# Order of the short sequence's attention blocks, stepwise block ends, and stores issued by POOL, in a one-layer bidirectional encoder

## The chip, the cores and the metric

The kernel runs on one core of one Trainium2 chip. The metric is the device time of one execution in microseconds (us); the median of several runs is given. The core has five engines that take their own instruction streams: PE (TensorE, matrix products, with its weight loads shown as PEld), DVE (VectorE), ACT (ScalarE), POOL (GpSimd) and SP (SyncE, which here only issues transfers). Transfers (DMA) are issued from the queues of SP, ACT and POOL. Engines wait for each other through semaphores.

## What is computed

One layer of a hybrid encoder over two sequences of 2048 and 256 positions with the same weights, in float32. Eight mLSTM heads (both directions) and eight attention heads (two key/value groups of four query heads) share one input projection:

```python
h = rmsnorm(x, norm1_w)
p = h @ w_in                       # mq, mk, mv, mo, gates, aq, ak, av
m_out = mlstm_mixer(mq, mk, mv, mo, gates, b_gates, mh_norm_w)
a_out = attention_mixer(aq, ak, av, q_norm_w, k_norm_w)
x = x + jnp.concatenate([m_out, a_out], axis=-1) @ w_out
h = rmsnorm(x, norm2_w)
a, g = jnp.split(centred_dwconv(h @ w_up, conv_w, conv_b), 2, axis=-1)
x = x + (jax.nn.silu(g) * a) @ w_down          # then a final rmsnorm
```

Attention is softmax(q k / 8) v without a mask, each sequence by itself. D = 1024, head width 64, feed-forward width 2816.

## The kernel before

Positions are cut into 18 tiles of 128: tiles 0 to 15 are the long sequence, 16 and 17 the short one. Every float32 product is made of two or three faster products of split operands: a "hi" part, and a "lo" part that holds what is left (DVE computes it as the difference).

Four stages follow each other. First comes the norm and the projection of what attention and the gates need (to about 260 us). Then attention and mLSTM run interleaved; when mLSTM is at its end (about 1385 us) the output projection with `w_out` takes its place beside attention (`phase_c`: nine blocks of 256 positions, each 192 matmuls `po`). Last comes the feed-forward part, from about 1870 us. The order of the instructions on each engine is fixed when the program is built: the kernel is written as generators that yield between steps, `run_both` takes steps of attention and of mLSTM by their cost, and a scheduler that comes with the language then places each engine's instructions by its own simulation of time. So an edit in one generator shifts instructions of others.

Attention (L461 to L677) works in 36 blocks, listed in `hbs`: a block is 512 queries (four tiles) of one key/value group. In group 0 a large block is four tiles of one head of the long sequence (16 blocks); in group 1 it is two tiles of two heads (16 blocks). Each group has two short blocks: both tiles of the short sequence for two heads. A large block passes over 16 key tiles in eight steps `kp` of two tiles, a short one over two key tiles in one step. Per block:

- `prep` (L529): loads the rotated queries (`bq`, by SP), turns them on PE (`pq`) and copies them to `qq` and `qm`.
- `maxstep` (L553): one matmul `px` of a query tile with up to 512 keys and its row maximum on DVE (`mx`, L558); 16 of them for a large block, 4 for a short one. `prep2` (L560) then writes the negative maximum into `qm`, through a PE transposition `pr`.
- `scores` (L573): per key tile two matmuls `ps`, two exponentials on ACT (`ph` L584, `ps` L585) and the lo part on DVE (`pl`, L586).
- `values` (L590): six matmuls into `pv`, two steps behind `scores`.
- `fin1` (L601): ACT copies `pv` to `o1` and `rs`. `fin2` (L610), four times: DVE takes the reciprocal of 128 columns of `rs`. `fin3` (L617): POOL multiplies and stores the block to `mix_d` (two stores for two heads, one for one). `fin4`: marks query tiles as done, which `run_both` asks before it hands out a block of the output projection.

While block n runs, block n+1 (`nxt`) is prepared, and block n−1 (`old`) is ended: one `fin2` per step, `fin3` at the sixth step, `fin4` at the last. A short block has one step, in which all four `fin2`, `fin3`, `fin4` of `old` and all of the preparation of the next block stand.

`mlstm` takes its heads in four pairs. `weights` (L692) loads eight tiles of 128×512 for pairs 1 to 3 (`rm`, SP), and ACT (L105) and DVE (L109) split each into hi and lo. Raw tiles come from two pools of two buffers. Its recurrence reads rows that were stored earlier (`dm`, POOL's loads from `nm_d`, with DMB buffers, L821).

`phase_c` (L960 to L1042): `loads` fetches the mixed heads (`cmx`, L988, split by ACT L989 and DVE L990) and x (`cx`, L994) by SP. `mm` makes `po` (L1003). `post` adds x (DVE, L1008), stores x1 (L1009, called `x_d` in the profile), and sums squares (ACT L1011, POOL L1013, `cacc`). `tail` makes the norm (DVE L1020) and stores it (L1022, `n_d`). In `loads`, `post` and `tail` SP issues all transfers, in program order. The last two blocks need the last attention block's output.

The feed-forward part reads `n_d` again (`rn`, `n`, `nt`, L1069 to L1090), loads the up weights (`ru`, L1103, split at L1115 and L1116; POOL's `tw`, L1124 to L1127, combines them), and multiplies on PE (`pa`, `pb`, `pc`, L1119).

Of the kernel before, what the change touches and what calls it, by code (L numbers as in the profile page):

```python
# [17 lines left out]
P = 128  # L18
# [6 lines left out]
HD = 64  # L25
# [30 lines left out]
WB = 8  # L56
RST = 512
QZB = 2
RWM = 4
S1B = 2  # L60
DMB = 6
KWB = 2
CSTEP = 1
LEAD = 1.3
# [47 lines left out]
def load_split(g, hi, lo, src, pool, name, step, col=None, bufs=2):  # L112

    n = src.shape[-1]
    for k in range(0, n, step):
        r = pool.tile([P, step], F32, tag="raw", name=f"{name}_{k}", bufs=bufs)
        split(g, hi[:, k:k + step], lo[:, k:k + step], src[:, k:k + step], r, col)
# [343 lines left out]
def attention(g, tc, s1, s2, pp):  # L461
# [5 lines left out]
    for grp in range(2):  # L467
        h0 = 4 * grp
        small = [(grp, [(h, 16, 18) for h in (hh, hh + 1)], 16, 18) for hh in (h0, h0 + 2)]
        if grp == 0:  # L470
            hbs += small + [(grp, [(h, 4 * b, 4 * b + 4)], 0, 16) for b in range(4) for h in range(h0, h0 + 4)]
        else:

            large = [(grp, [(h, 2 * b, 2 * b + 2) for h in (hh, hh + 1)], 0, 16) for b in range(8)
                     for hh in (h0, h0 + 2)]
            hbs += large[0:8] + small + large[8:]
    kv = {}

    def load_kv(grp, k0, k1, after=None):
# [49 lines left out]
    def prep(n):  # L529

        s = HB()
        grp, s.qs, k0, k1 = hbs[n]
        load_q(n)
        load_q(n + 1)
        load_kv(grp, k0, k1)
        s.kv = kv[(grp, k0)]
        s.nq, s.nk = 4, k1 - k0
        s.N = s.nq * P
        s.nm = "%d_%d" % s.qs[0][0:2]
        qz = qzs.pop(n)  # L540
        pq = pp.tile([P, 512], F32R, tag="sc", name="pq" + s.nm)
        for t in range(s.nq):
            nc.tensor.transpose(pq[:, t * P:(t + 1) * P], qz[:, t, :], g.identr)
        s.qq = sp.tile([P, 512], F32R, tag="qq", name="qq" + s.nm, bufs=2)
        nc.scalar.activation(s.qq[:, 0:s.N], f32(pq[:, 0:s.N]), AF.Copy)
        s.qm = sp.tile([65, 512], F32R, tag="qm", name="qm" + s.nm, bufs=2)
        nc.scalar.activation(s.qm[0:HD, 0:s.N], f32(pq[0:HD, 0:s.N]), AF.Copy)
        s.mx = sp.tile([P, 4, 4], F32, tag="mx", name="mx" + s.nm, bufs=2)
        s.nsp = -(-s.nk * P // 512)
        s.todo = [(t, z) for z in range(s.nsp) for t in range(s.nq)]  # L550
        return s

    def maxstep(s):  # L553
        t, z0 = s.todo.pop(0)
        w = min(512, s.nk * P - z0 * 512)
        ps = pp.tile([P, 512], F32, tag="sc", name=f"px{s.nm}_{t}_{z0}")
        nc.tensor.matmul(ps[:, 0:w], s.qq[:, t * P:(t + 1) * P], s.kv[z0][0][:, 0:w], start=True, stop=True)  # L557
        nc.vector.tensor_reduce(s.mx[:, t, z0:z0 + 1], ps[:, 0:w], AX.X, ALU.max)  # L558

    def prep2(s):  # L560

        nq = s.nq
        s.m4 = sp.tile([P, 4], F32, tag="m4", name="m4" + s.nm, bufs=2)
        nc.vector.tensor_reduce(s.m4[:, 0:nq], s.mx[:, 0:nq, 0:s.nsp], AX.X, ALU.max)
        m4r = sp.tile([P, 4], F32R, tag="m4r", name="m4r" + s.nm, bufs=2)
        nc.vector.tensor_scalar(m4r[:, 0:nq], s.m4[:, 0:nq], -1.0, None, ALU.mult)
        pr = pp.tile([P, 512], F32, tag="sc", name="pr" + s.nm)
        for t in range(nq):
            nc.tensor.matmul(pr[:, t * P:(t + 1) * P], m4r[:, t:t + 1].to_broadcast([P, P]), g.identr, start=True,
                             stop=True)  # L570
        nc.scalar.activation(s.qm[HD:HD + 1, 0:s.N], pr[HD:HD + 1, 0:s.N], AF.Copy)
# [29 lines left out]
    def fin1(s):  # L601

        N = s.N
        s.o1 = sp.tile([HD, 512], F32, tag="o1", name="o1" + s.nm, bufs=2)
        s.rs = sp.tile([HD, 512], F32, tag="rs", name="rs" + s.nm, bufs=1)
        nc.scalar.activation(s.o1[:, 0:N], s.pv[0:HD, 0:N], AF.Copy)
        nc.scalar.activation(s.rs[:, 0:N], s.pv[HD:P, 0:N], AF.Copy)
        s.left = list(range(0, N, P))

    def fin2(s):  # L610

        if s.left:
            r = s.rs[:, s.left[0]:s.left[0] + P]
            s.left.pop(0)
            nc.vector.reciprocal(r, r)

    def fin3(s):  # L617
        N = s.N
        nc.gpsimd.tensor_tensor(s.o1[:, 0:N], s.o1[:, 0:N], s.rs[:, 0:N], ALU.mult)
        for t0, (h, q0, q1) in part(s):  # L620
            r0 = HD * (h % 2)
            nc.gpsimd.dma_start(g.mix_d[q0 // 2:q1 // 2, r0:r0 + HD, 4 + h // 2].rearrange("n p t -> p n t"),
                                s.o1[:, t0 * P:(t0 + q1 - q0) * P].rearrange("p (n t) -> p n t", t=BT))

    def fin4(s):

        for h, q0, q1 in s.qs:
            if h == 7:
                g.mixed.update(range(q0, q1))
# [4 lines left out]
        yield 0.5  # L634
    prep2(cur)
    load_kv(0, 0, NT1, cur.m4)
    old = None
    for n in range(len(hbs)):
        nxt = prep(n + 1) if n + 1 < len(hbs) else None
        nkp = cur.nk // 2  # L640
        todo = []
        for kp in range(nkp):
            todo.append(scores(cur, kp))
            if kp >= PLAG:
                values(cur, *todo.pop(0))
            if nxt is not None and nxt.todo:
                if n == len(hbs) // 2 - 1:

                    k = 2 * (kp - 2) - (nxt.nq * nxt.nsp - len(nxt.todo))
                else:  # L650
                    k = -(-len(nxt.todo) // max(nkp - kp - MXE, 1))
                for _ in range(k):
                    maxstep(nxt)
                if not nxt.todo:
                    prep2(nxt)
            if old is not None:
                for _ in range(1 if kp < nkp - 1 else 4):
                    fin2(old)
                if kp == min(5, nkp - 1):
                    fin3(old)  # L660
                if kp == nkp - 1:
                    fin4(old)
                    old = None
            yield 2.2
        for t in todo:
            values(cur, *t)
        fin1(cur)
        yield 1
        if nxt is not None and nxt.todo:
            while nxt.todo:  # L670
                maxstep(nxt)
            prep2(nxt)
        old, cur = cur, nxt
    for _ in range(4):
        fin2(old)
    fin3(old)
    fin4(old)  # L677


def mlstm(g, tc, s1, sp, sw, sn, pj_, pm):  # L680
# [11 lines left out]
    def weights(p):  # L692
        s = Pair()
        s.p = p
        s.hs = slice(2 * p, 2 * p + 2)
        s.w = [sw.tile([P, 2, 512], F32R, tag="w", name=f"wm{p}_{c}", bufs=WB) for c in range(NCC)] if p else g.wm0
        for c in range(NCC if p else 0):
            load_split(g, s.w[c][:, 0, :], s.w[c][:, 1, :], g.w_m[p, c], g.raw if c % RWM < 2 else sp,
                       f"rm{p}_{c}", RST, g.n1w[:, c:c + 1], bufs=2 if c % RWM < 2 else RWM - 2)
        s.kT, s.qb, s.va, s.C, s.kw = [], [], [], [], {}  # L700
        for i in range(NT):
            s.C.append(sp.tile([P, 2, 65], F32, tag="C", name=f"C{p}_{i}", bufs=NT))
        for b in range(NB):
            s.kT.append(s1.tile([P, BT], F32, tag="kT", name=f"mkT{p}_{b}", bufs=NB))
            s.qb.append(s1.tile([P, 2, 2, P], F32, tag="qb", name=f"qb{p}_{b}", bufs=NB))
            s.va.append(s1.tile([P, 2, 2, 65], F32, tag="va", name=f"va{p}_{b}", bufs=NB))
        return s
# [252 lines left out]
def phase_c(g, sn, sp, pp, wps):  # L960
# [45 lines left out]

    def post(b, z, x, po, acc):
        nc.vector.tensor_tensor(x[z], po, x[z], ALU.add)  # L1008
        g.st.dma_start(g.x1_d[b, :, 2 * z:2 * z + 2], x[z])  # L1009
        q = acc if z == 0 else sp.tile([P, 2, BT], F32, tag="sq", name=f"csq{b}_{z}", bufs=1)  # L1010
        nc.scalar.activation(q, x[z], AF.Square, scale=1.0 / 32.0)  # L1011
        if z:
            nc.gpsimd.tensor_tensor(acc, acc, q, ALU.add)  # L1013

    def tail(b, x, acc):
        nc.gpsimd.tensor_tensor(acc[:, 0], acc[:, 0], acc[:, 1], ALU.add)
        r = rstd_bc(g, sp, pp, [acc[:, 0]], BT, "r", f"c{b}")
        for z in range(4):
            for o in range(2):
                nc.vector.scalar_tensor_tensor(x[z][:, o], x[z][:, o], g.n2w[:, 2 * z + o:2 * z + o + 1],  # L1020
                                               r, ALU.mult, ALU.mult)
            g.st.dma_start(g.n2_d[:, 2 * z:2 * z + 2, b * BT:(b + 1) * BT], x[z])  # L1022
        g.normed.add(b)

    for c in range(NCC):
# [491 lines left out]
```

## Time and profile before

| | us |
|---|---|
| runs, median of 3 (lowest, highest) | 3474.17 (3474.0, 3474.66) |
| the profiled execution: its own time | 3475.05 |
| its span in the profile | 3473.3 |
| PE busy in it | 3346.2 |
| DVE busy | 2670.5 |
| POOL busy | 1103.9 |

The profile is of one execution. Its own time is 1.75 us above its span. Views used below: the page itself; windows (busy time of each engine in a stretch of time, then the number of instructions in brackets); waits (which line of an engine waited for which other engine's line: total us, times, longest); groups (instructions of one line, one operation and one shape, with their number, total and mean in ns); transfers (number, KB, median us from issue to landing); and the timeline. In a name such as `po<-cmx,wo` the output stands left of the arrow.

### The profile page before, as it was taken

How to read it: one execution, taken by the hardware profiler on the slowest of the kernel's cores; microseconds unless marked ns; L12 is line 12 of the kernel's file. 1: busy time of each engine (PE TensorE's matmuls, PEld its weight loads, DVE VectorE, ACT ScalarE, POOL GpSimd, SP SyncE). 2: the span in 40 equal slices, each digit the busy share in tenths (PEclk: the TensorE clock that was granted, in tenths of full speed). 3: DMA queues.
4: the chain of work that ended last, by engine and by line, in shares of the span. 5: the costliest groups of instructions: out<-in, count | busy, mean ns of one | idle time of the engine just before them, and what ended most of it. 6: DMA issues, size and time to landing. Idle time of an engine off the chain costs nothing. (4 is left out here: it accounts for less than half of the span.)

```text
span 3473.3 us, 55765 instructions
## 1 busy us (share of the span) xinstructions
PE 3346.2 (96%) x20058; PEld 3103.0 (89%) x20058; DVE 2670.5 (77%) x4654; ACT 1930.9 (56%) x4329; POOL 1103.9 (32%) x1328
## 2 busy tenths in 40 slices
PE   7989999999999999999988999999999999999998
PEld 6878888888888887987778999999999998999998
DVE  6875687677777789767666888888888878887776
ACT  4536566666666766645554444446544446555555
POOL 6643133222224322211116233225333224322222
PEclk9999999999999999999999999999999999999999
DMA  6765334343355443432218233223333223421221
GB/s 222 238 197 162 117 107 118 104 131 101 105 169 161 131 144 115 145 105 70 68 51 296 73 97 98 74 65 130 127 105 99 67 73 119 145 65 63 73 73 50
DMA packets 258501, 404.29 MB, mean 116 GB/s; under 512 B 33552, under 2 KB 158256, under 8 KB 258224
## 3 DMA queue, kind: packets, MB, share of 16 engines
q1 hardware_dynamic: 230320, 358.24, 32.3%
q0 software_dynamic: 11344, 33.04, 3.5%
q10 hardware_dynamic: 16560, 9.44, 0.9%
q8 instruction: 158, 2.59, 0.3%
q14 instruction: 119, 0.97, 0.1%
HBM read 316.73 MB, written 83.90 MB: 115 GB/s over the span
## 5 line engine op out<-in xcount | busy, mean ns | idle before, releaser
L1257 PE MATMUL pd<-act,wd 128*128 128x384 f32 (+1 forms) x3120 | 593.2, 336 | 25.2 <-DVE acc L1259 14.4
L1257 PEld LDWEIGHTS pd<-act,wd 128*128 128x128 f32 x3120 | 539.5, 189 | 34.0 <-DVE acc L1259 20.0
L586 DVE TENSOR_TENSOR pl<-ps,ph 128x512 fp32r<-128x512 f32 x520 | 354.1, 685 | 235.3 <-ACT ps L585 228.2
L1119 PE MATMUL pa<-nt,wut 128*128 128x386 f32 (+2 forms) x2376 | 454.5, 339 | 2.0 <-DVE nt L1071 2.0
L1119 PEld LDWEIGHTS pa<-nt,wut 128*128 128x128 f32 x2376 | 421.4, 190 | 2.3 <-DVE nt L1071 2.3
L584 ACT ACTIVATE ph<-ps 128x512 fp32r<-128x512 f32 x520 | 309.7, 596 | 177.1 <-PE ps L581 172.3
L558 DVE TENSOR_REDUCE mx<-px 128x1 f32<-128x512 f32 (+1 forms) x528 | 343.8, 671 | 67.4 <-PE px L557 65.4
L1213 DVE SCALAR_TENSOR_TENSOR y<-u,cw,y 128x768 f32<-128x768 f32 (+1 forms) x264 | 314.0, 1190 | 36.3 <-ACT y L1206 29.2
L598 PE MATMUL pv<-ph,v 128*128 128x512 f32 (+1 forms) x1040 | 330.2, 405 | 2.9 <-ACT ph L584 2.4
L1124 POOL TENSOR_TENSOR tw<-ru 128x512 f32<-128x512 f32 x66 | 91.1, 1380 | 744.4 <-DMA ru<-w_up 573.3
L1135 ACT ACTIVATE u<-pa 128x386 f32<-128x386 f32 (+2 forms) x264 | 128.4, 486 | 328.4 <-PE pa L1119 326.9
L585 ACT ACTIVATE ps<-ps 128x512 f32<-128x512 f32 x520 | 310.9, 599 | 0.0
L1259 DVE TENSOR_TENSOR acc<-pd,acc 128x384 f32<-128x384 f32 (+1 forms) x544 | 280.6, 536 | 34.5 <-PE pd L1257 33.5
L1003 PEld LDWEIGHTS po<-cmx,wo 128*128 128x128 f32 x1728 | 233.9, 191 | 32.6 <-ACT cmx L989 16.2
L1003 PE MATMUL po<-cmx,wo 128*128 128x256 f32 x1728 | 242.2, 284 | 14.9 <-ACT cmx L989 14.8
L580 PE MATMUL ps<-qq,kk 128*128 128x512 f32 x520 | 217.0, 421 | 1.8 <-DVE pl L586 1.1
L557 PE MATMUL px<-kk,qq 128*128 128x512 f32 (+1 forms) x528 | 207.7, 411 | 6.6 <-DVE pl L586 3.5
L598 PE MATMUL pv<-pl,v 128*128 128x512 f32 x520 | 206.6, 407 | 6.9 <-DVE pl L586 6.6
L581 PE MATMUL ps<-qm,kl 65*128 65x512 f32 x520 | 209.1, 405 | 0.0
L724 PE MATMUL mj<-mn,wm 128*128 128x256 f32 x1296 | 197.4, 288 | 3.5 <-ACT og L738 2.1
L724 PEld LDWEIGHTS mj<-mn,wm 128*128 128x128 f32 x1296 | 182.1, 192 | 17.6 <-ACT og L738 2.5
L734 PE MATMUL mv<-wm,mn 128*128 128x256 f32 x1296 | 196.2, 288 | 1.1 <-ACT qb L730 0.9
(288 smaller groups left out, 7239.0 us busy)
## 6 DMA issues: line engine op xcount, KB each, us to landing
ru<-w_up SPq DMA_DIRECT2D x132, 512.0 KB, 3.4
mn<-n_d SPq DMA_DIRECT2D x216, 256.0 KB, 3.3
rd<-w_down SPq DMA_DIRECT2D x66, 512.0 KB, 3.6
n_d<-n1T SPq DMA_DIRECT2D x18, 1024.0 KB, 5.6
dm<-nm_d POOLq DMA_DIRECT2D x72, 256.0 KB, 4.0
mjn<-n_d SPq DMA_DIRECT2D x72, 256.0 KB, 3.3
mvn<-n_d SPq DMA_DIRECT2D x72, 256.0 KB, 3.2
q_d<-qz SPq DMA_DIRECT2D x18, 512.0 KB, 3.5
```

The costliest lines, as they stand in the source:

```text
L558: nc.vector.tensor_reduce(s.mx[:, t, z0:z0 + 1], ps[:, 0:w], AX.X, ALU.max)
L580: nc.tensor.matmul(ps, kk[:, kc:kc + P], s.qq[:, 0:N], start=True, stop=False)
L584: nc.scalar.activation(ph, ps, AF.Exp)
L585: nc.scalar.activation(ps, ps, AF.Exp)
L586: nc.vector.tensor_tensor(pl, ps, f32(ph), ALU.subtract)
L598: nc.tensor.matmul(s.pv[0:HD if k in (1, 3) else P, 0:N], v, p, start=(kp == 0 and k == 0), stop=(2 * kp + 2 == s.nk and k == 5))
L724: nc.tensor.matmul(pj[:, o], s.w[c][:, a, o * P:(o + 1) * P], nT[c][:, :, h, :], start=(c + o + k == 0), stop=(c == NCC - 1 and k == 2 and ...
L1003: nc.tensor.matmul(po[:, o], wo[c][z // 2][:, a, n], mx[c][:, h, :], start=(c == 0 and k == 0), stop=(c == NCC - 1 and k == 2))
L1119: nc.tensor.matmul(p, w[:, aa, c, :], ops[k][:, c, bb, 0:n], start=c == 0 and i == 0 and not add, stop=c == NCC // 2 - 1 and i == 2, skip_ ...
L1213: nc.vector.scalar_tensor_tensor(y[:, s:e], u[:, s + k:e + k], cw[:, k, jj:jj + 1], y[:, s:e], ALU.mult, ALU.add)
L1257: nc.tensor.matmul(po, wds[j][c // 4][:, aa, c % 4 * P:(c % 4 + 1) * P], acts[j][:, bb, z0:z1], start=(j == 0 and k == 0), stop=(j == len( ...
L1259: nc.vector.tensor_tensor(accs[c][:, z0:z1], po, accs[c][:, z0:z1], ALU.add)
```

## The change

The list `hbs` now has single short blocks between large ones. In group 0: short, large, short, then the other 15 large. In group 1: six large, short, two large, short, the other eight large. A list `ready` holds the prepared blocks; when the next block is short and the current one large, the block after the next is prepared too, both within the current block's steps. The block ends become a list `ends` of six steps per block (four `fin2`, `fin3`, `fin4`), of which one is done per step, two if more than six are left; so `fin3` stands at the fifth step and `fin4` at the sixth. `qq`, `qm`, `mx`, `m4` and `m4r` get a third buffer and `rs` a second. The `dm` buffers go from six to five, and mLSTM's raw weight tiles from two pools of two buffers to the one pool of two. The two stores of `phase_c` (x1 and its norm, 36 each) are issued by POOL instead of SP (`g.st` is SP).

```diff
@@ -56,9 +56,8 @@
 WB = 8
 RST = 512
 QZB = 2
-RWM = 4
 S1B = 2
-DMB = 6
+DMB = 5
 KWB = 2
 CSTEP = 1
 LEAD = 1.3
@@ -468,12 +467,13 @@
         h0 = 4 * grp
         small = [(grp, [(h, 16, 18) for h in (hh, hh + 1)], 16, 18) for hh in (h0, h0 + 2)]
         if grp == 0:
-            hbs += small + [(grp, [(h, 4 * b, 4 * b + 4)], 0, 16) for b in range(4) for h in range(h0, h0 + 4)]
+            large = [(grp, [(h, 4 * b, 4 * b + 4)], 0, 16) for b in range(4) for h in range(h0, h0 + 4)]
+            hbs += small[0:1] + large[0:1] + small[1:] + large[1:]
         else:
 
             large = [(grp, [(h, 2 * b, 2 * b + 2) for h in (hh, hh + 1)], 0, 16) for b in range(8)
                      for hh in (h0, h0 + 2)]
-            hbs += large[0:8] + small + large[8:]
+            hbs += large[0:6] + small[0:1] + large[6:8] + small[1:] + large[8:]
     kv = {}
 
     def load_kv(grp, k0, k1, after=None):
@@ -541,11 +541,11 @@
         pq = pp.tile([P, 512], F32R, tag="sc", name="pq" + s.nm)
         for t in range(s.nq):
             nc.tensor.transpose(pq[:, t * P:(t + 1) * P], qz[:, t, :], g.identr)
-        s.qq = sp.tile([P, 512], F32R, tag="qq", name="qq" + s.nm, bufs=2)
+        s.qq = sp.tile([P, 512], F32R, tag="qq", name="qq" + s.nm, bufs=3)
         nc.scalar.activation(s.qq[:, 0:s.N], f32(pq[:, 0:s.N]), AF.Copy)
-        s.qm = sp.tile([65, 512], F32R, tag="qm", name="qm" + s.nm, bufs=2)
+        s.qm = sp.tile([65, 512], F32R, tag="qm", name="qm" + s.nm, bufs=3)
         nc.scalar.activation(s.qm[0:HD, 0:s.N], f32(pq[0:HD, 0:s.N]), AF.Copy)
-        s.mx = sp.tile([P, 4, 4], F32, tag="mx", name="mx" + s.nm, bufs=2)
+        s.mx = sp.tile([P, 4, 4], F32, tag="mx", name="mx" + s.nm, bufs=3)
         s.nsp = -(-s.nk * P // 512)
         s.todo = [(t, z) for z in range(s.nsp) for t in range(s.nq)]
         return s
@@ -560,9 +560,9 @@
     def prep2(s):
 
         nq = s.nq
-        s.m4 = sp.tile([P, 4], F32, tag="m4", name="m4" + s.nm, bufs=2)
+        s.m4 = sp.tile([P, 4], F32, tag="m4", name="m4" + s.nm, bufs=3)
         nc.vector.tensor_reduce(s.m4[:, 0:nq], s.mx[:, 0:nq, 0:s.nsp], AX.X, ALU.max)
-        m4r = sp.tile([P, 4], F32R, tag="m4r", name="m4r" + s.nm, bufs=2)
+        m4r = sp.tile([P, 4], F32R, tag="m4r", name="m4r" + s.nm, bufs=3)
         nc.vector.tensor_scalar(m4r[:, 0:nq], s.m4[:, 0:nq], -1.0, None, ALU.mult)
         pr = pp.tile([P, 512], F32, tag="sc", name="pr" + s.nm)
         for t in range(nq):
@@ -602,7 +602,7 @@
 
         N = s.N
         s.o1 = sp.tile([HD, 512], F32, tag="o1", name="o1" + s.nm, bufs=2)
-        s.rs = sp.tile([HD, 512], F32, tag="rs", name="rs" + s.nm, bufs=1)
+        s.rs = sp.tile([HD, 512], F32, tag="rs", name="rs" + s.nm, bufs=2)
         nc.scalar.activation(s.o1[:, 0:N], s.pv[0:HD, 0:N], AF.Copy)
         nc.scalar.activation(s.rs[:, 0:N], s.pv[HD:P, 0:N], AF.Copy)
         s.left = list(range(0, N, P))
@@ -634,47 +634,52 @@
         yield 0.5
     prep2(cur)
     load_kv(0, 0, NT1, cur.m4)
-    old = None
+    ends = []
+    ready = [cur]
+
+    def end(s):
+
+        return [lambda: fin2(s)] * 4 + [lambda: fin3(s), lambda: fin4(s)]
+
     for n in range(len(hbs)):
-        nxt = prep(n + 1) if n + 1 < len(hbs) else None
+        cur = ready.pop(0)
+
+        while n + len(ready) + 1 < len(hbs) and (not ready or len(ready) == 1 and ready[0].nk < 4 and cur.nk > 4):
+            ready.append(prep(n + len(ready) + 1))
         nkp = cur.nk // 2
         todo = []
         for kp in range(nkp):
             todo.append(scores(cur, kp))
             if kp >= PLAG:
                 values(cur, *todo.pop(0))
-            if nxt is not None and nxt.todo:
+            left = sum(len(s.todo) for s in ready)
+            if left:
                 if n == len(hbs) // 2 - 1:
 
-                    k = 2 * (kp - 2) - (nxt.nq * nxt.nsp - len(nxt.todo))
+                    k = 2 * (kp - 2) - (ready[0].nq * ready[0].nsp - left)
                 else:
-                    k = -(-len(nxt.todo) // max(nkp - kp - MXE, 1))
+                    k = -(-left // max(nkp - kp - MXE, 1))
                 for _ in range(k):
-                    maxstep(nxt)
-                if not nxt.todo:
-                    prep2(nxt)
-            if old is not None:
-                for _ in range(1 if kp < nkp - 1 else 4):
-                    fin2(old)
-                if kp == min(5, nkp - 1):
-                    fin3(old)
-                if kp == nkp - 1:
-                    fin4(old)
-                    old = None
+                    s = next(s for s in ready if s.todo)
+                    maxstep(s)
+                    if not s.todo:
+                        prep2(s)
+            for _ in range(2 if len(ends) > 6 else 1):
+                if ends:
+                    ends.pop(0)()
             yield 2.2
-        for t in todo:
-            values(cur, *t)
+        for x in todo:
+            values(cur, *x)
         fin1(cur)
+        ends += end(cur)
         yield 1
-        if nxt is not None and nxt.todo:
-            while nxt.todo:
-                maxstep(nxt)
-            prep2(nxt)
-        old, cur = cur, nxt
-    for _ in range(4):
-        fin2(old)
-    fin3(old)
-    fin4(old)
+        for s in ready:
+            if s.todo:
+                while s.todo:
+                    maxstep(s)
+                prep2(s)
+    for f in ends:
+        f()
 
 
 def mlstm(g, tc, s1, sp, sw, sn, pj_, pm):
@@ -695,8 +700,8 @@
         s.hs = slice(2 * p, 2 * p + 2)
         s.w = [sw.tile([P, 2, 512], F32R, tag="w", name=f"wm{p}_{c}", bufs=WB) for c in range(NCC)] if p else g.wm0
         for c in range(NCC if p else 0):
-            load_split(g, s.w[c][:, 0, :], s.w[c][:, 1, :], g.w_m[p, c], g.raw if c % RWM < 2 else sp,
-                       f"rm{p}_{c}", RST, g.n1w[:, c:c + 1], bufs=2 if c % RWM < 2 else RWM - 2)
+            load_split(g, s.w[c][:, 0, :], s.w[c][:, 1, :], g.w_m[p, c], g.raw,
+                       f"rm{p}_{c}", RST, g.n1w[:, c:c + 1])
         s.kT, s.qb, s.va, s.C, s.kw = [], [], [], [], {}
         for i in range(NT):
             s.C.append(sp.tile([P, 2, 65], F32, tag="C", name=f"C{p}_{i}", bufs=NT))
@@ -1006,7 +1011,7 @@
 
     def post(b, z, x, po, acc):
         nc.vector.tensor_tensor(x[z], po, x[z], ALU.add)
-        g.st.dma_start(g.x1_d[b, :, 2 * z:2 * z + 2], x[z])
+        nc.gpsimd.dma_start(g.x1_d[b, :, 2 * z:2 * z + 2], x[z])
         q = acc if z == 0 else sp.tile([P, 2, BT], F32, tag="sq", name=f"csq{b}_{z}", bufs=1)
         nc.scalar.activation(q, x[z], AF.Square, scale=1.0 / 32.0)
         if z:
@@ -1019,7 +1024,7 @@
             for o in range(2):
                 nc.vector.scalar_tensor_tensor(x[z][:, o], x[z][:, o], g.n2w[:, 2 * z + o:2 * z + o + 1],
                                                r, ALU.mult, ALU.mult)
-            g.st.dma_start(g.n2_d[:, 2 * z:2 * z + 2, b * BT:(b + 1) * BT], x[z])
+            nc.gpsimd.dma_start(g.n2_d[:, 2 * z:2 * z + 2, b * BT:(b + 1) * BT], x[z])
         g.normed.add(b)
 
     for c in range(NCC):
```

## The prediction

> **What bounds the kernel now.** I read the page first, then the busy time by stage, then PE's waits and SP's waits, then the groups of instructions.
>
> ```profile
> span 3473.3 us, 55765 instructions
> PE 3346.2 (96%) x20058; PEld 3103.0 (89%) x20058; DVE 2670.5 (77%) x4654; ACT 1930.9 (56%) x4329; POOL 1103.9 (32%) x1328
> 500.00:750.00 250.00, 249.44 (x1617) 220.89 (x1616) 181.38 (x401) 164.35 (x449) 61.08 (x126) 1.00 0.39 113
> 1250.00:1425.00 175.00, 167.15 (x1003) 140.56 (x1002) 145.22 (x350) 116.20 (x304) 44.36 (x84) 0.98 0.45 132
> 1425.00:1550.00 125.00, 125.00 (x874) 114.33 (x873) 88.97 (x160) 59.60 (x119) 27.80 (x28) 1.00 0.38 116
> 1550.00:1800.00 250.00, 232.12 (x1250) 187.14 (x1249) 171.12 (x297) 138.92 (x272) 30.36 (x33) 0.96 0.20 61
> 1800.00:1925.00 125.00, 107.08 (x702) 103.77 (x701) 81.78 (x110) 58.60 (x103) 64.98 (x52) 0.93 0.69 230
> ```
>
> TensorE (PE) is the bound: 3346.2 of 3473.3 us, so 127 us of idle is all that any reordering can touch. The window rows show start and end, then the width, then busy time of PE, its weight loads, DVE, ACT and POOL, then the granted clock and DMA share. The change reorders 260 to 1900 us. Of that, 500 to 750 has 0.6 us of PE idle, and 1425 to 1550, where the short sequence's blocks of the second head group run between projection matmuls, has none at all. What idles is 1250–1425 (7.9 us), 1550–1800 (17.9) and 1800–1925 (17.9).
>
> ```profile
> PE po L1003 <- ACT cmx L989: 14.8, 3, 13.9
> PE pa L1119 <- DVE wu L1116: 2.0, 1, 2.0
> SPq L1009 <- DVE cx L1008: 94.4, 21, 11.6
> SPq L1022 <- DVE cx L1020: 65.8, 24, 16.5
> ```
>
> The first two are PE's waits over the whole span (total, times, longest), the others the SP queue's from 1350 to 1900 us. The two stores that move to POOL (L1009, L1022) hold SP for 160 us; but PE's waits for what SP loads behind them are 14.8 us, and 13.9 of those are one wait, the last projection blocks' for attention's last output.
>
> **The change part by part**, against the profiled run's 3475.05 us (span 3473.3 and 1.75 around it; the runs' median is 0.9 below). PE, DVE and ACT keep the same number of instructions; 72 DMA issues go from SP to POOL. So only idle time can change. In the compiled order of the changed program PE's first 1201 steps (to about 262 us) and the final stage's are unmoved.
>
> *The short blocks.* Of the second head group's two short blocks, the first now stands before the seventh large block, inside the stage where mLSTM ends.
>
> ```profile
> 1331.00:1356.00 25.00, 23.95 (x154) 20.50 (x153) 20.91 (x57) 17.90 (x51) 6.39 (x12) 1.00 0.48 147
> 1356.00:1381.00 25.00, 20.98 (x91) 14.82 (x90) 24.50 (x62) 16.05 (x47) 5.49 (x9) 0.89 0.15 45
> L586 DVE TENSOR_TENSOR pl<-ps,ph 128x512 fp32r<-128x512 f32 x520 | 354.1, 685 | 235.3 <-ACT ps L585 228.2 <-PE ps L581 5.5
> L558 DVE TENSOR_REDUCE mx<-px 128x1 f32<-128x512 f32 x512 | 337.4, 680 | 61.9 <-PE px L557 60.2
> L615 DVE RECIPROCAL rs<-rs 64x128 f32<-64x128 f32 x144 | 121.8, 898 | 5.0 <-ACT rs L607 4.9
> L580 PE MATMUL ps<-qq,kk 128*128 128x512 f32 x520 | 217.0, 421 | 1.8 <-DVE pl L586 1.1
> L598 PE MATMUL pv<-ph,v 128*128 128x512 f32 x520 | 213.3, 410 | 2.9 <-ACT ph L584 2.4 <-ACT rs L607 0.2
> L598 PE MATMUL pv<-pl,v 128*128 128x512 f32 x520 | 206.6, 407 | 6.9 <-DVE pl L586 6.6
> L557 PE MATMUL px<-kk,qq 128*128 128x512 f32 x512 | 203.5, 414 | 6.6 <-DVE pl L586 3.5 <-DVE mx L558 2.4
> ```
>
> At 1356 to 1381 DVE is busy 24.50 of 25 us and PE 20.98: here DVE is the bound. One short block brings DVE 2 pl, 4 mx and 4 reciprocals: 2×0.685 + 4×0.680 + 4×0.898 = 7.7 us. PE's part is at most 2×(0.421+0.410+0.407) + 4×0.414 = 4.1. So the stage grows by 3.6 us where PE's part is worked off meanwhile, by 7.7 where it is not, and by nothing if the scheduler lets mLSTM's DVE work slide behind it into 1425–1550, where DVE has 36 us free. In the compiled order almost nothing but attention stands on PE around this block (the next block's scores and maxima), so I take **+5 (0 to +7.7)**. Before, the block cost PE no idle, so nothing is gained where it left. The projection that filled it (73 and 198 matmuls around the two short blocks) fills the large ones instead. By the orders, the first of the last seven large blocks has 67 projection matmuls instead of 117 and the five after it have nearly the same as before (98, 94, 107, 85, 106 against 98, 94, 109, 83, 108), so their 17.9 us of idle stays; what ran in the one block runs earlier beside full PE: **−1 (−4 to +3)**.
>
> At the start, the first large block is prepared within the first short block instead of the second, one block earlier, and this needs all the long sequence's keys sooner:
>
> ```profile
> kk<-k_d POOLq DMA_DIRECT2D x16, 128.0 KB, 3.3
> x_d<-cx SPq DMA_DIRECT2D x36, 256.0 KB, 2.6
> n_d<-cx SPq DMA_DIRECT2D x36, 256.0 KB, 2.3
> dm<-nm_d POOLq DMA_DIRECT2D x72, 256.0 KB, 4.0
> mix_d<-mmx SPq DMA_DIRECT2D x18, 64.0 KB, 1.6
> mix_d<-o POOLq DMA_DIRECT2D x40, 64.0 KB, 2.2
> rm<-w_m SPq DMA_DIRECT2D x32, 256.0 KB, 5.0
> L622 POOL DMA_DIRECT2D mix_d<-o x56 | 33.1, 593 | 9.2 <-POOL o L619 9.2
> ```
>
> The last number of a DMA row is us from issue to landing. A key tile late by one landing costs 3.3; the other work of PE there covers most: **+1 (0 to +3.3)**.
>
> *Ends step by step, more buffers (2 to 3, 1 to 2).* The four reciprocals stay one per step; the multiply and the mix_d stores come one or two steps earlier (the multiply at the fifth step instead of the sixth, the stores at the sixth instead of the eighth). They are off PE's path but for the last block, whose chain is below. **0.** Five dm buffers instead of six cost a wait only if POOL's dm loads (4.0 us) run more than five ahead; I take it at 0, covered by PE's projection in 300–1000, and up to 3 if not.
>
> *mLSTM's weights through two raw buffers instead of four.* Per change of head pair, 8 tiles:
>
> ```profile
> L105 ACT ACTIVATE wm<-rm,nw x8: 722/724/739, 703.4 to 716.8; 128x512 fp32r<-128x512 f32 x8
> L109 DVE SCALAR_TENSOR_TENSOR wm<-rm,nw,wm x8: 739/746/753, 704.7 to 717.6; 128x512 fp32r<-128x512 f32 x8
> DMA to landing us min/median/max: 2.7/5.0/7.1
> ```
>
> Before, the eight took 703.4 to 718.3. With two buffers there are four rounds of a load (5.0) and the two splits (0.72 + 0.75), three of them after the first: 3 × 6.5 + 1.5 = 21 us instead of 15. At the landings' extremes it is 14 to 27, so −1 to +12 a change. The compiled order puts other PE work of 20, 13 and 16 us between the last use of the old tile and the first of the new; only the second is short, by some 3 us once landing jitter is allowed: **+2 (0 to +6)**.
>
> *The stores by POOL.* 72 issues × 0.593 = 43 us of POOL's time, where POOL is busy 30 of 250 us (1550–1800): hidden. A POOL issue that waits for DVE's add (L1008) holds what is behind it on POOL: multiply L619, the mix_d stores, cacc, dm. Nothing of these is near PE's path, since mix_d is read a block later. SP's freed 160 us make cmx, cx and bq loads earlier, worth at most PE's 14.8 − 13.9 = 0.9: **−0.5**.
>
> At the end of the projection:
>
> ```profile
> 1814.89 3.22 DVE L1020 SCALAR_TENSOR_TENSOR cx<-cx,nw,rs_c 128x256 f32<-128x256 f32 x8 [3.25 <-PE rs_c L134]
> 1818.03 3.37 DVE L615 RECIPROCAL rs<-rs 64x128 f32<-64x128 f32 x4
> 1821.53 1.25 POOL L619 TENSOR_TENSOR o<-o,rs 64x512 f32<-64x512 f32 x1 [10.00 <-DVE rs L615]
> 1823.08 1.14 POOL L622 DMA_DIRECT2D mix_d<-o  x2 [0.29 <-POOL o L619]
> 1829.02 3.39 PE L1003 MATMUL po<-cmx,wo 128*128 128x256 f32 x14 [13.93 <-ACT cmx L989]
> ...
> 1889.65 2.71 SPq L1022 DMA_DIRECT2D n_d<-cx  x4
> 1892.64 0.35 SPq L1103 DMA_DIRECT2D ru<-w_up  x1
> ```
>
> These are from the timeline (start, duration, in brackets the idle before). Eight norm multiplies, four reciprocals, the multiply, two stores, their load: the same links remain, so the 13.9 us stays. If the n2 stores stand ahead of the two mix_d issues on POOL it is up to 4 × 0.593 = +2.4; if DVE's order is better, −2: **0**. At the start of the final stage the up-projection's weight load (1892.64) no longer stands behind four n_d stores (1889.65) on SP, which removes the 2.0 us wait of pa on wu; in their place n2 stores leave POOL, 16 issues × 0.593 = 9.5 us between POOL's own work, and land later by up to 4.0 − 2.3 = 1.7: **−1.5 (−2 to +3)**.
>
> Here a rule weighs against the change. The row: POOL's 64 KB stores land in 2.2 us, SP's in 1.6; nothing in the trace shows one stuck behind DVE. The Trainium skill ("SBUF — State Buffer", section "SBUF: two separate sides", the box on DVE blocking DMA) says that a DMA issued from POOL has its descriptors written by GpSimd's cores, which cannot do it while DVE runs a fast two-port operation. By the rule each issue could stretch to a DVE operation's length, and the term of the final stage's start would be +3.4 instead of −1.5.
>
> **Sum:** +5 − 1 + 1 + 0 + 2 − 0.5 + 0 − 1.5 = +5 us; 3475.05 + 5 = 3480.05 as a profiled run, **3479** as a median of runs. That is within 0.2% (±6.95 us, 3467.2 to 3481.1), which is what a measurement can tell from no change.
>
> **The rivals.**
>
> *Slower: the backlog is paid in full.* The mechanism is DVE's backlog at the end of mLSTM, which pushes the block behind the short one, whose own preparation (16 mx × 0.68 = 10.9 us) is now due earlier too. 7.7 + 10.9 = 18.6 of DVE work ahead of PE, of which PE's own part of the short block (4.1) runs meanwhile: +14, so 3488. It decides once DVE's work per block passes PE's. For it: DVE busy 24.50 of 25. Against it: DVE's 36 us free right after.
>
> *Faster: SP's freed time spreads the projection.* If loads run ahead, projection matmuls fall into 1550–1800 at the granted clock of 1.00 rather than 0.96: 17.9 of idle, less 4 that the order leaves anyway: −14, so 3460. For it: 160 us of SP waits. Against it: the order of PE there is fixed and hardly altered.
>
> *POOL's stores lengthen.* At 0.898 (a reciprocal) instead of 0.593 a store, the 16 at the final stage's start cost 16 × 0.305 = 4.9 more on POOL, ahead of its own part of the final stage: 3479 + 4.9 = 3484. This is what the Trainium skill's box would make of it.
>
> *It does nothing.* The short blocks had no PE idle to remove (125.00 of 125 in 1425–1550), and every added term is covered: 3474 ± 2.
>
> **How the numbers follow.** Forecast 0.38 (of it 0.08 above 3481.1), nothing 0.09, full backlog 0.21, POOL's stores 0.06, faster 0.26. So faster 0.26, same 0.30 + 0.09 = 0.39, slower 0.08 + 0.21 + 0.06 = 0.35. The forecast's own range is 3470 to 3487, its terms' ends taken together fewer than all at once; for 8 in 10 the range reaches to the cases on both sides: 3460 to 3491.
>
> **What would show it.** PE idle in 1250–1425 rises from 7.9 to about 13, with DVE full to past 1400; 1550–1800 keeps about 18; the wait of po on cmx stays near 14; pa's on wu is gone; near 705 to 725 PE waits once on the weights' split; POOL's x_d and n_d stores land in 3 to 4 us. Wrong if PE idle in 1550–1800 falls by more than 5 (faster rival), or if PE waits appear on mN, mI or dm in 300–1250 where I put none: that would mean the new order hurts mLSTM, which no row of before prices.

## The result and the profile after

The changed kernel takes 3486.07 us (median of 6 runs, 3481.46 to 3488.8), the kernel before, run on the same chips, 3473.77 (3470.79 to 3474.66). The ratio is 1.0038, with a 95% interval of 1.0027 to 1.005: slower by about 12 us. The profiled run of the changed kernel took 3488.8 us, 13.75 more than the one before. After line 636 the changed file's lines stand five further down (L1003 is L1008, L1020 is L1025).

The page and the windows of the changed kernel (span; busy time; then stages: width, busy time of PE, PEld, DVE, ACT, POOL, granted clock, DMA share, GB/s):

```profile
span 3487.1 us, 55921 instructions
PE 3354.8 (96%) x20058; PEld 3108.3 (89%) x20058; DVE 2693.5 (77%) x4654; ACT 1933.5 (55%) x4329; POOL 1156.5 (33%) x1400
500.00:750.00 250.00, 248.86 (x1625) 221.31 (x1625) 185.47 (x414) 164.91 (x456) 68.08 (x144) 1.00 0.38 114
1250.00:1425.00 175.00, 165.61 (x988) 140.11 (x988) 140.35 (x330) 114.57 (x292) 44.15 (x80) 0.96 0.43 131
1425.00:1550.00 125.00, 124.92 (x860) 113.34 (x859) 85.52 (x154) 63.18 (x126) 39.03 (x48) 1.00 0.36 113
1550.00:1800.00 250.00, 232.94 (x1220) 185.71 (x1219) 175.07 (x295) 136.36 (x264) 46.24 (x58) 0.94 0.19 57
1800.00:1925.00 125.00, 101.03 (x659) 94.71 (x658) 85.62 (x106) 53.12 (x96) 76.47 (x75) 0.92 0.68 227
```

The stages up to 1800 us look alike: 9.4 us of PE idle in 1250–1425 instead of 7.9, 17.1 in 1550–1800 instead of 17.9. The stage that stands out is the last: 24.0 us of idle in 1800–1925 instead of 17.9. PE's waits from 1800 to 1950 us in the changed kernel:

```profile
PE po L1008 <- ACT cmx L994: 12.5, 1, 12.5
PE pc L1124 <- ACT u L1140: 6.5, 1, 6.5
PE pb L1124 <- DVE wu L1121: 1.5, 1, 1.5
PE pc L1124 <- DVE nt L1076: 1.3, 1, 1.3
PE pa L1124 <- DVE nt L1076: 0.9, 1, 0.9
PE pa L1124 <- DVE wu L1121: 0.9, 2, 0.6
```

The wait for attention's last output is what it was (12.5 after 13.9). Behind it, at the start of the feed-forward stage, PE waits 11 us, where it waited 4.0 before; a new wait of 6.5 us leads, of `pc` on ACT's `u`, the copy that takes an earlier product out of its buffer. The waits are not the whole price. From the start of the last `po` to the first `pd` (the first matmul with the down weights) PE is idle for 4.0 us before and 11.5 after, and busy for 45.6 and 48.5 with as many matmuls; the granted clock of this stretch is 0.97 and 0.91, and from 1923 to 1928 us, right behind the long wait, it is 0.50. To see why `u` was late, follow the last projection block through the engines, in the timeline of the changed kernel (start, duration; rows left out are marked):

```profile
1880.39 4.57 DVE L1314 TENSOR_TENSOR wd<-rd,wd 128x512 fp32r<-128x512 f32 x2 [1.28 <-ACT wd L1313]
1884.89 0.68 DVE L1013 TENSOR_TENSOR cx<-po,cx 128x512 f32<-128x512 f32 x1
...
1886.45 1.74 POOL L1018 TENSOR_TENSOR cacc<-cacc,csq 128x512 f32<-128x512 f32 x1
1888.16 1.72 POOL L1132 TENSOR_TENSOR tw<-ru,tw 128x512 f32<-128x512 f32 x1
1889.85 4.23 POOL L1076 TENSOR_TENSOR nt<-nt 128x772 fp32r<-128x772 f32 x2
1894.04 1.46 POOL L1021 TENSOR_TENSOR cacc<-cacc 128x256 f32<-128x256 f32 x1
...
1901.62 0.50 PE L127 MATMUL rs_c<-ones,cacc 128*128 128x2 f32 x4
...
1909.13 3.21 DVE L1025 SCALAR_TENSOR_TENSOR cx<-cx,nw,rs_c 128x256 f32<-128x256 f32 x8
1910.30 3.06 POOL L1027 DMA_DIRECT2D n_d<-cx  x4
...
1915.07 0.63 ACT L1120 ACTIVATE wut<-tw 128x512 fp32r<-128x512 f32 x1 [2.27 <-PE pa L1124]
1916.88 0.63 ACT L1120 ACTIVATE wut<-ru 128x512 fp32r<-128x512 f32 x1 [1.18 <-PE pb L1124]
1917.42 1.93 ACT L1211 ACTIVATE y<-u,cw 128x768 f32<-128x768 f32 x2
...
1922.06 0.84 ACT L1292 ACTIVATE y<-y 128x768 f32<-128x768 f32 x1 [1.42 <-DVE y L1218]
1922.81 0.47 ACT L1140 ACTIVATE u<-pc 128x386 f32<-128x386 f32 x1
1923.34 4.23 PE L1124 MATMUL pc<-n,wu 128*128 128x386 f32 x12 [6.54 <-ACT u L1140]
```

The same block in the kernel before:

```profile
1871.87 2.39 DVE L1309 TENSOR_TENSOR wd<-rd,wd 128x512 fp32r<-128x512 f32 x2 [1.69 <-ACT wd L1308]
1874.19 0.68 DVE L1008 TENSOR_TENSOR cx<-po,cx 128x512 f32<-128x512 f32 x1
...
1875.67 1.29 POOL L1013 TENSOR_TENSOR cacc<-cacc,csq 128x512 f32<-128x512 f32 x1 [1.95 <-ACT csq L1011]
1877.04 1.07 POOL L1016 TENSOR_TENSOR cacc<-cacc 128x256 f32<-128x256 f32 x1
...
1879.10 0.50 PE L128 MATMUL rs_c<-ones,cacc 128*128 128x2 f32 x4
...
1888.76 3.22 DVE L1020 SCALAR_TENSOR_TENSOR cx<-cx,nw,rs_c 128x256 f32<-128x256 f32 x8 [2.12 <-PE rs_c L134]
1896.30 1.95 ACT L1206 ACTIVATE y<-u,cw 128x768 f32<-128x768 f32 x2
```

Before, the block's last sum (`cacc`, 128x256) follows its predecessor at once. After, its inputs are ready at 1888.2, but three other POOL operations (tw, nt, nt) stand in front, and it starts at 1894.0. None of these POOL rows shows a wait: it is the order that the scheduler wrote for POOL. The norm, its four stores, the first `y` of the feed-forward stage and, behind `y` on ACT, `u<-pc` all come later in turn. Counted from the start of the last `po` (1872.4 before, 1879.0 after; these 6.6 us are taken up with the short block's term below), the norm starts 16.3 us after it before and 30.2 after, `y` 23.9 and 38.4, the first `pd` 49.6 and 60.0.

POOL's queue is not the whole of the norm's 14 us. The last add on DVE (`cx<-po,cx`) already starts 5.9 us after the last `po` instead of 1.8, behind two splits of `wd` that take 4.57 us instead of 2.39: 4.1 us. Between its two sums POOL loses 6.2. PE takes the finished sum up (`rs_c<-ones,cacc`) 7.8 us after the last sum starts instead of 2.3: 5.5. From there to the norm the changed kernel is 2.1 faster. Neither the last add nor POOL's last sum nor this matmul shows a wait of its own in the changed kernel, so the new order of DVE and PE takes its part as well as POOL's.

### The profile page after: what moved, and what is told of

The parts are those of the page before. It is cut to its first block, busy times and chain, and to the rows that moved or that the text cites. A ratio compares the mean times of both kernels' runs of the same rounds, so it can differ in the third digit from the quotient of the medians.

```text
span 3487.1 us, 55921 instructions
## 1 busy us (share of the span) xinstructions
PE 3354.8 (96%) x20058; PEld 3108.3 (89%) x20058; DVE 2693.5 (77%) x4654; ACT 1933.5 (55%) x4329; POOL 1156.5 (33%) x1400
## 5 line engine op out<-in xcount | busy, mean ns | idle before, releaser
L1008 PEld LDWEIGHTS po<-cmx,wo 128*128 128x128 f32 x1728 | 232.3, 192 | 29.4 <-ACT cmx L994 13.3
L1008 PE MATMUL po<-cmx,wo 128*128 128x256 f32 x1728 | 241.5, 284 | 13.6 <-ACT cmx L994 12.7
L739 PEld LDWEIGHTS mv<-wm,mn 128*128 128x128 f32 x1296 | 182.0, 190 | 16.3 <-ACT qb L735 1.4
```

Of the source, the lines that this page charges most:

```text
L1008: nc.tensor.matmul(po[:, o], wo[c][z // 2][:, a, n], mx[c][:, h, :], start=(c == 0 and k == 0), stop=(c == NCC - 1 and k == 2))
```

## The experiments

Twelve variants were run; each time is compared with the kernel before, run beside it. The three offsets are read from the timeline of each one's profile and counted, as above, from the start of its last `po`, in us; they place the loss, which the whole time alone cannot.

| kernel | ratio to before (95% interval) | norm | y | first pd |
|---|---|---|---|---|
| before | 1 | 16.3 | 23.9 | 49.6 |
| changed | 1.0038 (1.0027, 1.005) | 30.2 | 38.4 | 60.0 |
| changed, both stores by SP | 1.0002 (0.9993, 1.0011) | 17.6 | 25.2 | 50.7 |
| before, both stores by POOL | 1.0026 (1.0015, 1.0037) | 31.5 | 39.0 | 60.4 |
| changed, old block order | 1.003 (1.0022, 1.0039) | 31.6 | 38.6 | 60.5 |
| before, fewer buffers | 1.0001 (0.9992, 1.0009) | 16.9 | 24.4 | 52.0 |
| changed, only x1 by POOL | 1.0015 (1.0006, 1.0024) | 21.9 | 28.6 | 55.5 |
| changed, only the norm by POOL | 1.002 (1.0011, 1.0029) | 27.1 | 34.4 | 56.2 |
| changed, blocks 7 and 8 by SP | 1.0001 (0.9992, 1.001) | 15.7 | 23.2 | 50.3 |
| before, blocks 7 and 8 by POOL | 1.004 (1.0026, 1.0053) | 32.6 | 40.9 | 61.2 |
| changed, block 8 by SP | 1.0011 (1.0003, 1.002) | 30.4 | 34.4 | 53.8 |
| changed, last sums by DVE | 1.0015 (1.0006, 1.0023) | 21.0 | 27.7 | 54.7 |
| before, last sums by DVE | 0.9992 (0.9983, 1.0001) | 12.9 | 21.3 | 47.1 |
| before, block 8 ahead of 7 | 1.0041 (1.0029, 1.0054) | 13.5 | 40.4 | 69.8 |

**The parts of the change, one at a time.** Three theories stood against each other: POOL's stores (A), the order of the short blocks (B), the buffers (C). The changed kernel with both stores by SP:

```diff
-        nc.gpsimd.dma_start(g.x1_d[b, :, 2 * z:2 * z + 2], x[z])
+        g.st.dma_start(g.x1_d[b, :, 2 * z:2 * z + 2], x[z])
...
-            nc.gpsimd.dma_start(g.n2_d[:, 2 * z:2 * z + 2, b * BT:(b + 1) * BT], x[z])
+            g.st.dma_start(g.n2_d[:, 2 * z:2 * z + 2, b * BT:(b + 1) * BT], x[z])
```

> The changed kernel, x1 and norm stores by SP again; all else as changed. The changed kernel is 12.3 us above the one before. Theory A (POOL's stores): most of the loss is at the start of the final stage, where PE's waits rose from 4.0 to 12.0 us and the first pd came 10 us later relative to the last pv; then this is 8 to 11 us faster than the changed kernel, about 3476 to 3478, and the first pd follows the first pa by about 50 us instead of 60. Theory B (short blocks' order): this stays within 3 us of the changed kernel, 3483 to 3488.

It took 3473.99 us: the whole loss is gone, to within the interval. The reverse edit, made to the kernel before:

> The kernel before, with only the x1 and norm stores moved to POOL. PE's order changes only after about 1400 us. Theory A: 8 to 11 us slower than before, 3482 to 3485, and the loss stands between the first pa and the first pd. Theory B: within 3 us of before.

3481.93 us, ratio 1.0026 (about 9 us), with the new wait in the same place. PE's waits of this variant from 1800 to 1950 us:

```profile
PE po L1003 <- ACT cmx L989: 13.0, 1, 13.0
PE pc L1119 <- ACT u L1135: 5.7, 1, 5.7
PE pc L1119 <- DVE nt L1071: 3.1, 1, 3.1
```

Neither the block order nor the buffers are needed for the loss. The next two say the same from the other side. The block list of before, put into the changed kernel:

```diff
-            hbs += small[0:1] + large[0:1] + small[1:] + large[1:]
+            hbs += small + large
...
-            hbs += large[0:6] + small[0:1] + large[6:8] + small[1:] + large[8:]
+            hbs += large[0:8] + small + large[8:]
```

> The changed kernel with the block list of before (short blocks in pairs); stepwise ends, buffers and POOL stores as changed. Theory B: the loss ahead of the final stage (last pv 6.5 us later) goes: about 3479 to 3480. Theory A: as slow as the changed kernel, 3483 to 3488. If the buffers are the cause (theory C) it also stays slow, but ahead of the last pv.

3482.11 us: it stays slow. And the fewer buffers alone (DMB = 5, mLSTM's raw tiles all from `g.raw`) in the kernel before:

> The kernel before with five dm buffers and mLSTM's raw weight tiles from one pool of two. Theory C (buffers): 3 to 8 us slower than before, with PE waits on the weights' split near 420, 705 and 985 us. Theories A and B: within 3 us of before (my own term for it was +2, 0 to +6).

3473.64 us, ratio 1.0001. Theory C falls, theory A stands, and of B no more than a few us can be left.

**Which of the stores.** From the changed kernel, only the norm's store back on SP, then only x1's:

> The changed kernel with only the norm's store (L1027) back on SP; x1's store stays with POOL. Theory A-n (the last block's norm and its stores on POOL: POOL's order puts the block's last sum and its rstd behind the n and nt splits, and the norm's four stores behind a whole set of tw): the loss is gone, 3474 to 3477 as with both on SP, first pd about 50 us after first pa. Theory A-x (an x1 store that waits for DVE ahead of POOL's sums) or theory A-all (43 us of POOL issues spread over the projection): half the loss or more stays, 3479 to 3484.

> The changed kernel with only x1's store (L1014) back on SP; the norm's store stays with POOL. Theory A-n: the whole loss stays, 8 to 11 us above the variant with both stores on SP, first pd about 60 us after first pa, and a PE wait of pc on ACT's u of 5 to 7 us. Theory A-x: 3474 to 3477. Theory A-all: about half, 3478 to 3480.

The theory of the norm's stores alone missed, and so did that of x1's. With x1 alone on POOL 4.6 us remain (3478.4 against 3473.82), with the norm alone 4.5 (3478.3), by the ratios 5 and 7; each pushes the norm later than before, by 6 and by 11 us, and the first `pd` by 6 and by 7. So it isn't one kind of store, and such parts are also what a cost spread over all 72 issues would give. The next kernel tells place from number: stores by POOL for blocks 0 to 6 and by SP for 7 and 8,

```diff
-        nc.gpsimd.dma_start(g.x1_d[b, :, 2 * z:2 * z + 2], x[z])
+        (nc.gpsimd if b < 7 else g.st).dma_start(g.x1_d[b, :, 2 * z:2 * z + 2], x[z])
```

and the same for the norm's:

> The changed kernel with both stores by POOL for projection blocks 0 to 6 and by SP for the last two, 7 and 8. Theory A-n: the loss is gone, 3474 to 3477, though 56 of the 72 issues stay with POOL. Theory A-all: most of the loss stays, 3481 to 3485.

3474.03 us, ratio 1.0001, though 56 of 72 issues stay with POOL. The block's last sum is back behind its predecessor, in the timeline of this variant:

```profile
1879.13 1.29 POOL L1018 TENSOR_TENSOR cacc<-cacc,csq 128x512 f32<-128x512 f32 x1 [1.96 <-ACT csq L1016]
1880.50 1.07 POOL L1021 TENSOR_TENSOR cacc<-cacc 128x256 f32<-128x256 f32 x1
...
1890.65 3.22 DVE L1025 SCALAR_TENSOR_TENSOR cx<-cx,nw,rs_c 128x256 f32<-128x256 f32 x8 [0.55 <-PE rs_c L133]
1898.19 1.95 ACT L1211 ACTIVATE y<-u,cw 128x768 f32<-128x768 f32 x2
```

The reverse, in the kernel before only blocks 7 and 8 by POOL:

> The kernel before with both stores by POOL for projection blocks 7 and 8 alone (16 of 72 issues). Theories Q and L: the whole loss of the variant with all 72 by POOL, 8 to 10 us slower than before, first pd about 60 us after first pa. If the 56 others carry part of the loss, 3 to 5 us.

3484.96 us, ratio 1.004: these 16 stores alone cost as much as all 72. The other 56 cost nothing that can be measured (the interval of the variant above ends at 1.001, 3.5 us).

**Queue or landing.** Two ways are open by which 16 stores do this: they push POOL's other work back (Q), or they land late and `y` waits for them (L). Block 8's stores by SP, block 7's by POOL:

> The changed kernel with the stores of the last block (8) by SP and of all others, block 7 too, by POOL. Theory Q: block 7's four norm stores stand on POOL in the middle of block 8's sums, and the norm comes late all the same: 4 to 8 us above the variant with both blocks on SP, first pd 54 to 58 us after first pa. Theory L: only block 8's stores can hold y, so the loss is gone, 3474 to 3477, first pd 50 us after first pa.

3478.32 us, ratio 1.0011, 4.1 above before: theory L alone falls, since no store of block 8 is left on POOL and the norm is as late as with all of them (30.4). But it is cheaper than the changed kernel, and a row of ACT in this variant shows what `y` can wait for:

```profile
1905.07 3.21 DVE L1025 SCALAR_TENSOR_TENSOR cx<-cx,nw,rs_c 128x256 f32<-128x256 f32 x8
1905.96 2.71 SPq L1027 DMA_DIRECT2D n_d<-cx  x4
1909.05 1.96 ACT L1211 ACTIVATE y<-u,cw 128x768 f32<-128x768 f32 x2 [0.28 <-DMA n_d<-cx]
```

Here `y` does wait for a store of the norm, for 0.28 us: the projection's pools are closed before the main part of the feed-forward stage begins, and its tiles take their place. It starts 4.0 us after the norm begins. In the changed kernel it starts 8.3 us after, but no wait for a store is seen there: the second of the four stores, whose landing at 1908.9 lets `y` go here, has landed there at 1914.1 us, 3.3 us before `y` starts, and on ACT two splits of `wut` stand ahead of `y` that wait for PE's `pa` and `pb`. So what is shown is a late norm and, in the changed kernel, a new order on ACT too; that a store's landing holds `y` for longer than 0.28 us is not shown. The next kernel leaves all stores with POOL and takes the last two blocks' sums off it:

```diff
-            nc.gpsimd.tensor_tensor(acc, acc, q, ALU.add)
+            (nc.gpsimd if b < 7 else nc.vector).tensor_tensor(acc, acc, q, ALU.add)
...
-        nc.gpsimd.tensor_tensor(acc[:, 0], acc[:, 0], acc[:, 1], ALU.add)
+        (nc.gpsimd if b < 7 else nc.vector).tensor_tensor(acc[:, 0], acc[:, 0], acc[:, 1], ALU.add)
```

> The changed kernel, all 72 stores by POOL, but the sums of squares of the last two projection blocks (L1018, L1021) added by DVE instead of POOL. Theory Q (the stores push POOL's share of the last block's norm behind other POOL work, in the order that the scheduler writes; the norm then comes late, and the final stage's first y and u with it): with the sums off POOL the norm's eight multiplies start about 16 us after the first pa again (30 in the changed kernel), first pd 50 to 53 us after first pa (60), time 3474 to 3478. Theory L (the stores themselves land late from POOL, and y waits for their landing): first pd stays 58 to 60 us after first pa, 3482 to 3487.

3477.14 us, ratio 1.0015, the norm at 21.0 and the first `pd` at 54.7 (counted from the last `po`; one `pa` stands ahead of the last `po` here). That is about half of the loss recovered with no store moved, and fits the parts above: POOL no longer stands between the sums, but the last add itself (L1013) still comes late, 6.0 us after the start of the last `po` instead of 1.8. The queue theory, which expected the norm at about 16 and the first `pd` at 50 to 53, is right about the place and too strong about the amount. The control, the same sums on DVE in the kernel before:

> Control: the kernel before (stores by SP) with the same sums on DVE. If the move is worth something by itself, this is faster than before by the same amount; theory Q expects within 3 us of before, first pd 49 to 52 us after first pa.

3470.1 us against 3474.25, ratio 0.9992 with an interval that just reaches 1.0001. The norm starts 3.4 us earlier and the first `pd` 2.5. It is the only variant whose median lies below before, but a gain is not established.

**A way to do better that failed.** The 13.9 us wait for attention's last output is the longest in both kernels. Block 8 belongs to the short sequence, whose heads are done long before, so it was put ahead of block 7 in the kernel before:

```diff
-    for b in range(NB):
+    for i, b in enumerate((0, 1, 2, 3, 4, 5, 6, 8, 7)):
```

(with the buffers alternating by i).

> The kernel before with the last two projection blocks exchanged: block 8 (the short sequence, whose heads are done at about 1456 us) ahead of block 7, which needs attention's last output. Some 150 of block 8's 192 po (0.118 us each, 17.7 us) stand after the last pv. If the 13.9 us wait of po on cmx is due only to the order of the blocks, it goes, and the time falls by 9 to 14 us, to about 3460. If projection matmuls that filled attention's last blocks are lacking there instead, PE idle moves into 1550 to 1800 and the gain is under 5 us.

3487.37 us, ratio 1.0041: slower. The wait of `po` on cmx went, and the last `po` started at 1865.4 instead of 1872.4, but from then to 1883.1 PE had only the norm's eight small matmuls. PE in this variant:

```profile
1853.58 12.12 PE L1003 MATMUL po<-cmx,wo 128*128 128x256 f32 x99
1873.79 1.01 PE L128 MATMUL rs_c<-ones,cacc 128*128 128x2 f32 x4 [8.09 <-POOL cacc L1016]
1876.78 1.23 PE L134 MATMUL rs_c<-ident,rcol_c 128*128 128x128 f32 x4 [1.98 <-POOL rcol_c L132]
1883.10 1.01 PE L1119 MATMUL pa<-n,wu 128*128 128x386 f32 x2 [5.09 <-ACT wu L1115]
```

The first load of the up weights, in the kernel before and in this variant:

```profile
1851.76 0.33 SPq L1102 DMA_DIRECT2D ru<-w_up  x1
1876.55 0.46 SPq L1102 DMA_DIRECT2D ru<-w_up  x1
```

In the kernel before, the feed-forward stage's first loads and splits (rn, n, ru, wu) ran almost wholly behind the 13.9 us wait (the first split starts at 1830 us), beside the `po` of the last two blocks; the first `ru` was issued 21 us ahead of the first `pa`. In the variant it is issued 11 us after the last `po`, the sum of the last block takes until 1873.7, and PE waits for both. Why the scheduler puts `ru` that late is not shown.

## Why the prediction was right or wrong

The time lay in the range (3460 to 3491) and above the likeliest case (3479, within 0.2%); the case that came was slower by over 0.2%, though not by the mechanism that the slower rival named. That the range holds it is luck: its upper part was there for DVE's backlog, which did not happen, and the term that grew was summed at −1.5.

- *The start of the final stage, −1.5 (−2 to +3):* this step failed. It measured +10.4 (first `pd` at 60.0 instead of 49.6), and 60.0 to 61.2 in all four kernels that have both stores of blocks 7 and 8 and the sums on POOL. I priced 16 issues by their duration and by their landing, and looked for who waits for the landing. I did not ask what else POOL does in the block's own chain: sum, rstd, then the norm that is to be stored. The change put the stores on the engine that makes them possible, and the scheduler wrote another order for it. Why sixteen stores make it write this order is not shown. The wait of `pa` on wu, which I let go, was to be the gain: it went from 2.0 to 0.9, and waits of 11 us in all took the place of 4.0.
- *"So only idle time can change":* this premise failed too. Of the 10.4 us, 7.5 are idle time and 2.9 are the same matmuls at a lower granted clock. Over the whole span of the two profiles PE's busy time rose by 8.6 us (3346.2 to 3354.8), its idle time by 5.2.
- *The stores by POOL, hidden:* right for 56 of the 72, shown by the variant with blocks 7 and 8 on SP. Their issues cost 0.57 and 0.74 us, near the 0.593 assumed, and land in 2.7 and 3.0 us instead of 2.6 and 2.3 by SP. In the rows of the groups and of the transfers in the changed kernel:

```profile
L1027 POOL DMA_DIRECT2D n_d<-cx x36 | 26.4, 735 | 33.5 <-DVE cx L1025 29.5 <-issue 3.1
L1014 POOL DMA_DIRECT2D x_d<-cx x36 | 20.5, 568 | 155.6 <-DVE cx L1013 91.0 <-DVE m4r L566 42.1 <-DMA cx<-xT 16.6
x_d<-cx POOLq DMA_DIRECT2D x36, 256.0 KB, 2.7
n_d<-cx POOLq DMA_DIRECT2D x36, 256.0 KB, 3.0
SPq L999 <- DMA n_d<-cx: 125.5, 17, 22.0
SPq L993 <- PE po L1008: 118.1, 30, 32.9
```

  The rival of longer issues named the right stage, at half the price, for a reason that these rows don't bear out: the issues took 0.57 and 0.74 us on the mean, not 0.898. The Trainium skill ("SBUF — State Buffer", "SBUF: two separate sides") ties the starving of such stores to fast two-port operations of DVE. No starved store is seen here; whether any such operation ran beside these stores no run shows. The last two rows, SP's waits from 1350 to 1900 us, show where SP's freed time (160 us of waits) went: it now waits for the same stores to land, before it may load x again, and for `po`.
- *The short block in the DVE-bound stage, +5 (0 to +7.7):* not settled between 0 and about 4. Both variants with the new order and SP's last stores stand at 1.0002 and 1.0001, with intervals up to 1.0011 (3.8 us). In the profiles the last `po` starts at 1877.2 on the mean of the seven with the new order and at 1872.5 on the six with the old one (without the exchanged blocks), 4.7 later; each group spreads over 6 us, and only one profile of the old order lies among those of the new. But it isn't idle time, as forecast: up to there PE is idle for 81.5 us on the mean with the new order and 82.7 with the old one, and busy for 1795.7 and 1789.8. The 1250–1425 idle rose by 1.5, not by 5, while the granted clock fell from 0.98 to 0.96 there and from 0.96 to 0.94 in 1550–1800. That the whole time does not show these 5 us stays open. The full-backlog rival did not happen.
- *mLSTM's weights, +2 (0 to +6):* the splits take as long as worked out, but PE hardly waits for them: once, 0.6 us, and at the third change of head pair instead of the second. The rows of the tile `rm` and its splits from 690 to 740 us in the changed kernel:

```profile
L104 ACT ACTIVATE wm<-rm,nw x8: 708/722/726, 691.3 to 709.8; 128x512 fp32r<-128x512 f32 x8
L108 DVE SCALAR_TENSOR_TENSOR wm<-rm,nw,wm x8: 741/748/1181, 692.0 to 711.5; 128x512 fp32r<-128x512 f32 x8
```

  From 691.3 to 712.3 it is 21 us, as forecast, instead of 15; they start 12 us earlier than before, and PE's idle from 500 to 750 us is 1.1 instead of 0.6. That the 21 fits is partly luck, since the loads landed in 3.2 us here and not in the 5.0 of the working. The buffers alone measured 1.0001 (0.9992 to 1.0009), so the term is 0 to within 3 us.
- *The wait for attention's last output, 0:* right, 12.5 instead of 13.9.
- *The faster rival:* projection matmuls did not move into 1550–1800; its idle stayed (17.1), as the compiled order said.
- *The other terms:* they were not measured one by one; the changed kernel with both stores by SP holds them all and stands at 1.0002. The working puts the `mix_d` stores at the sixth step instead of the eighth, but in `fin3` they stand with the multiply, at the fifth instead of the sixth. Of the sign that the new order hurts mLSTM, waits on mN or dm in 300–1250, 1.6 us appear in the changed kernel (0.6 before).

## What to carry to other kernels

Before a store is moved to another engine's queue, list what that engine does on the chain that leads to the store and on the chain that its release lets go, at the place where little else covers PE: here sixteen issues counted there, and fifty-six elsewhere didn't. Where a scheduler writes the order, read the new order of that engine, and of those that take turns with it, around the end of each stage, instead of pricing the issues one by one. Removing a long wait pays only if the next stage's loads and splits still find matmuls to run beside.

## What the runs showed of the hardware that was not expected

The changes leave PE's work in the feed-forward stage alone, and yet it (first `pd` to PE's last matmul) took 1533.1 to 1543.5 us in the profiles of the fourteen kernels. One profile can't place a change of the whole time below some 10 us, and offsets within a stage can.

A wait of PE cost more than its length here. Behind the 6.5 us wait in the changed kernel twelve `pc` took 4.23 us, where the next twelve of the same operands, at 1939.3, took 2.28; the granted clock was 0.50 from 1923 to 1928 us and 1.00 again from 1933 to 1938.
